# Hybrid encoder layer on one core: probability transposes issued in pairs of groups, gate transposes at the end of an iteration and in another PSUM bank pool

## The chip, the cores and the metric

One Trainium2 chip, one of its cores. The time is device microseconds for one execution of the whole kernel: one layer over 4096 tokens of width 1024. The engines are PE (TensorE, matmuls), DVE (VectorE), ACT (ScalarE), POOL (GpSimd) and SP (SyncE, which here only issues transfers). Each takes its own instructions in the order in which the built program lists them.

## The reference, cut to what matters

```python
h = rms(x) * norm_gain * (1 + scale) + shift          # scale, shift, gate = Linear(SiLU(c))
q, k, v, g_attn, u, v_gm, g_gm = split(h @ w_in)      # 8 query heads, 2 key/value heads of 64
s = rms(q) @ rms(k).T / 8 - slope * dist              # band of +-128 tokens, blocks of 128 queries
A = softmax([s, sink])[..., :-1] @ v * silu(g_attn)
M = u * (w_s @ rms(v_gm) + b_s) * silu(g_gm)          # chunks of 128 tokens
x = x + gate * (concat[A, M] @ w_out)
```

Float32 operands are split into a high and a low part (`h` and `l` in names), so that each product is three matmuls: high by high, low by high, high by low.

## The kernel before, in words

The work is done in three phases. Phase 1 makes query, key, value and attention gate of each of 32 blocks of 128 tokens and does the attention; it writes the attention half of the transposed, gated result to HBM. Phase 2 does the gMLP half, phase 3 the output product. The change touches phase 1 only.

Phase 1 is a loop, `run_iter(i)`, whose steady iterations are alike. The main work of iteration i is the projection of block i on PE: 24 matmuls of 256 columns for key and value (`pk`), 24 of 512 columns for the query (`pq`) and 24 of 512 for the gate (`pg`). Between them, `sides1(i)` inserts the attention of block a = i - 3 and preparations of other blocks. Each inserted step has a position, a fraction of the main work by the table `TUNE`; steps are sorted by position and issued when the main work has come that far.

The steps that matter here, for block a:

- `qk`, eight heads: two matmuls of 384 columns into a score tile `s` of the PSUM pool "s" (two banks); a DVE instruction at L551 adds the mask and takes the minimum (`mx`); ACT takes the exponential (L555). After the fourth and the eighth head `softmax` makes the denominators of those four on DVE (`es`, `den`, and the reciprocal at L568), and POOL scales the four probability tiles `pr` by them (L571).
- `pt_`, six groups, one for each key/value head j and key block q: four transposes on PE of four scaled probability tiles into one tile `pT` of the PSUM pool "t" (two banks), then ACT copies it to `ph` (L580) and DVE makes the rest `pl` (L581), which frees the bank.
- `pv_`, six groups: two matmuls of 512 columns that add probabilities times values into `po` of the pool "o".
- `tr_g`: four transposes of the gate tile `gf` into `gT`, before the change in a bank of the pool "s"; `finish1` multiplies the result `y` by it (L604), which frees that bank, and sends `y` to HBM from SP.
- `tr_q`, `tr_k` for block i - 1: four transposes of the query (`pqT`, pool "s") and one of the key (`pkT`, pool "t").
- `bg_bias2`, in 24 iterations: SP loads 256 KB of weights (`bgw`, L620) and DVE adds it, scaled, to a bias that phase 2 needs (L625 the first three times, L627 after that). It belongs to no block.

A scheduler then orders each engine's instructions by priority, which follows the order of issue in the code, and by its own estimate of when the inputs of each are there. So a step that moves on one engine can change the order on others. From iteration 29 on the PE's instructions are kept in the order of the code.

Of the kernel before, what the change touches and what calls it, by code (L numbers as in the profile page):

```python
# [8 lines left out]
F32 = mybir.dt.float32  # L9
# [7 lines left out]
P = 128  # L17
# [18 lines left out]
TUNE = dict(pin0=4, pin1=4, pinx=1, pinb=1, sqb=2, gfb=3, pk=3, pq=0, pg=0, bg0=4, vm=[[], ["v0", "v1", "g0", "g1",  # L36
            "v2"], ["v3", "g2", "g3"]], wg0=1.05, wgd=0.18, vn=0, vx=0.2, wv0=0.145, wvd=0.15,
            silu=0.45, ksplit=2, sb=["q1", "g0", "g1", "q0", "q2", "g2"], ch0=28, load=0.02, split=0.0,
            stats=0.525, bg=0.1, qk0=0.08, qkd=0.035, pt0=0.485, ptd=0.0715, pvlag=0.31, trg=0.5,
            fin=0.99, trk=0.93, trq=0.9, order="kqg", unch=0, hp2=30, hpx=0, qeng="V")  # L40


def body(tc, x, xT, c, cT, w_adaT, b_adaT, w_gate, b_gate, ngT, w_in, q_gain, k_gain, sink, wsT, bsT, w_out, out):
    nc = tc.nc
    V, A, G, T = nc.vector, nc.scalar, nc.gpsimd, nc.tensor
# [17 lines left out]
    def tr(ps, src):  # L63
        pe(T.transpose(ps, src, ident))  # L64
# [37 lines left out]
    def load_xT(pool, b, bufs=2, tail=False):  # L102
# [5 lines left out]
    ps_mm, ps_s, ps_t, ps_o = (  # L108
        ctx.enter_context(tc.tile_pool(name=f"ps_{t}", bufs=2, space=PSUM)) for t in ("mm", "s", "t", "o")
    )  # L110
# [165 lines left out]
    with tc.tile_pool(name="start", bufs=1) as st:  # L276
# [107 lines left out]
        for k in range(KC):  # L384
# [4 lines left out]
            t = base.tile([P, DA], F32, tag="qf", name=f"tg{k}", bufs=2)  # L389
# [131 lines left out]
    def slots(b):  # L521
        by = {(b + r) % 3: b + r for r in (-1, 0, 1) if 0 <= b + r < NB}
        s = sorted(by)
        assert s[-1] - s[0] + 1 == len(s)
        return by, s[0], s[-1] + 1
# [47 lines left out]
    def pt_(b, j, a):  # L573
        d = blk[b]
        pt = ps_t.tile([P, QPK, P], F32, tag="t", name=f"pT{b}_{j}_{a}")
        for i in range(QPK):
            tr(pt[:, i], d["pr", j][i][:, a])
        ph = base.tile([P, QPK, P], F32R, tag="ph", name=f"ph{b}_{j}_{a}", bufs=4)
        pl = base.tile([P, QPK, P], F32R, tag="pl", name=f"pl{b}_{j}_{a}", bufs=4)
        A.copy(ph, pt)  # L580
        V.tensor_tensor(pl, pt, ph.bitcast(F32), ALU.subtract)  # L581
        d["p", j, a] = ph, pl
# [19 lines left out]
    def finish1(b):  # L602
        d = blk[b]
        V.tensor_tensor(d["y"], d["y"], d["pg"], ALU.mult)  # L604
        (nc.scalar if b == NB - 1 else nc.sync).dma_start(yT[b][0], d["y"])

    def tr_g(b):
        d = blk[b]
        pt = ps_s.tile([P, 4, P], F32, tag="s", name=f"gT{b}")
        for i in range(4):  # L610
            tr(pt[:, i], d["gf"][:, i * P : (i + 1) * P])
        d["pg"] = pt
# [22 lines left out]
    def sides1(i):  # L635
        s = []

        def add(pos, f):
            s.append((pos, len(s), f))
# [12 lines left out]
        a = i - LAG  # L652
        if 0 <= a < NB:
            for b in range(NB):
                if i == max(b + LAG - 1, NS):
                    add(TUNE["silu"] if b > 1 else 0.0, lambda b=b: silu1([b]))
            _, s0, s1 = slots(a)
            for h in range(NH):
                add(TUNE["qk0"] + TUNE["qkd"] * h, lambda h=h: qk(a, h))
            seq = [(j, q) for j in range(NKV) for q in range(s0, s1)]  # L660
            for n, (j, q) in enumerate(seq):
                add(TUNE["pt0"] + TUNE["ptd"] * n, lambda j=j, q=q: pt_(a, j, q))
                add(TUNE["pt0"] + TUNE["ptd"] * n + TUNE["pvlag"], lambda j=j, q=q: pv_(a, j, q))
            add(TUNE["trg"], lambda: tr_g(a))
            add(max(TUNE["fin"], TUNE["pt0"] + TUNE["ptd"] * 5 + TUNE["pvlag"] + 0.001), lambda: finish1(a))
# [532 lines left out]
```

## Time and profile before

| | us |
|---|---|
| median of 3 runs | 1734.18 (1733.92 to 1738.13) |
| the profiled execution | 1734.84 |
| its span, first to last instruction | 1733.1 |
| phase 1, steady iterations (block 4 on) | from 113.0 on, 23.6 each |
| first matmul of phase 2's products inside the loop's tail | 783.7 |

Mean granted TensorE clock 0.990. Times in the rows below count from the start of the span. A row of the timeline is one instruction, or several equal ones in a row; matmul ends are modelled, so neighbouring matmuls overlap, and the pace of PE is read from start to start. The iteration shown below is that of block 23, from 562.19 to 585.82, with the attention of block 20.

### The profile page before, as it was taken

Reading aid. Unit: us, or ns where it says so; the run is one execution under the profiler, and the core shown is the slowest. Engines: PE = TensorE matmul, PEld = TensorE weight load, DVE = VectorE, ACT = ScalarE, POOL = GpSimd, SP = SyncE. Lnnn points to the kernel's source line nnn. Section 1 sums busy time; section 2 is a strip of 40 time slices with the busy share of each in tenths; the row PEclk is TensorE's granted clock in tenths of the full one; section 3 lists DMA queues with packets and bytes.
Section 4 is the critical chain, followed back from the end, with each engine's and each line's share of the span. In section 5 each row is a group of like instructions: output and inputs, shape, how many; then the busy total and the mean of one; then the engine's idle time right before and its main releaser. Section 6 shows DMA issues by size and latency. Waiting matters only on the chain.

```text
span 1733.1 us, 23001 instructions
## 1 busy us (share of the span) xinstructions
PE 1659.0 (96%) x8216; PEld 1370.8 (79%) x8216; DVE 1069.3 (62%) x2277; ACT 739.2 (43%) x1613; POOL 690.9 (40%) x612
## 2 busy tenths in 40 slices
PE   6789999999999999998989999998999989999999
PEld 4578888888888888876778888887888867888887
DVE  7987877787877787769773333355333456444443
ACT  3476666666666666656421212211122233222221
POOL 5653343443343443346422222222222337545552
PEclk9899999999999999999999999999999999999999
DMA  7522212222212222113250101136111146555442
GB/s 259 192 85 74 73 45 67 74 74 74 73 43 69 73 74 92 37 55 100 74 192 25 61 25 61 49 127 225 37 49 61 61 177 200 163 164 184 146 148 83
DMA packets 67762, 170.92 MB, mean 99 GB/s; under 512 B 8256, under 2 KB 8256, under 8 KB 67648
## 3 DMA queue, kind: packets, MB, share of 16 engines
q1 hardware_dynamic: 62896, 160.81, 27.9%
q10 hardware_dynamic: 4752, 8.65, 1.3%
q8 instruction: 64, 1.05, 0.3%
q14 instruction: 50, 0.41, 0.1%
HBM read 128.54 MB, written 40.89 MB: 98 GB/s over the span
## 4 chain that ended last, share of the span: by engine, by line
PE 78%; DVE 10%; ACT 2%; DMA 1%; issue 1%; POOL 1%; SPq 0%; POOLq 0%; DVEq 0%; ACTq 0%
PE pg L61 17%; PE pv L61 9%; PE pu L61 9%; PE pq L61 9%; PE oY L967 7%; PE oX L967 5%; PE oZ L967 5%; PE pT L64 5%; PE s L61 5%; PE po L61 3%; DVE y L600 2%; DVE pr L551 1%; PE sv L61 1%; PE pk L61 1%; DVE gf L495 1%
## 5 line engine op out<-in xcount | busy, mean ns | idle before, releaser
L97 POOL TENSOR_TENSOR xl<-xraw,xh 128x1024 fp32r<-128x1024 f32 x58 | 150.6, 2596 | 377.4 <-ACT xh L96 377.4
L571 POOL TENSOR_SCALAR pr<-pr,den 128x384 f32<-128x384 f32 (+1 forms) x256 | 146.4, 590 | 160.9 <-DVE vs L445 105.3
L555 ACT ACTIVATE pr<-pr,mx 128x384 f32<-128x384 f32 (+1 forms) x256 | 153.8, 601 | 59.0 <-DVE mx L551 58.3
L580 ACT CAST ph<-pT 128x512 fp32r<-128x512 f32 x188 | 109.7, 584 | 117.2 <-PE po L61 43.0
L551 DVE CUSTOM_DVE_ANT_0 pr<-s,negd,nsink 128x384 f32<-128x384 f32 (+1 forms) x256 | 152.5, 607 | 11.5 <-PE s L61 6.0
L61 PE MATMUL pu<-w2u,xh 128*128 128x512 f32 x480 | 148.8, 391 | 0.0
L61 PE MATMUL s<-kT,qT 128*128 128x384 f32 (+1 forms) x512 | 135.7, 346 | 12.8 <-DVE mx L551 11.7
L581 DVE TENSOR_TENSOR pl<-pT,ph 128x512 fp32r<-128x512 f32 x188 | 126.0, 685 | 15.6 <-ACT ph L580 15.6
L83 POOL TENSOR_TENSOR ssv<-ssv,mhalf 128x8 f32<-128x8 f32 x32 | 53.6, 1675 | 177.4 <-DVE ssv L82 177.2
L64 PE MATMUL pT<-ident,pr 128*128 128x128 f32 x752 | 115.9, 274 | 4.8 <-DVE pl L581 3.1
L64 PEld LDWEIGHTS pT<-ident,pr 128*128 128x128 f32 x752 | 93.3, 140 | 34.3 <-POOL pr L571 6.6
L61 PEld LDWEIGHTS s<-kT,qT 128*128 128x128 f32 x512 | 86.3, 188 | 33.4 <-DVE mx L551 20.6
L96 ACT CAST xh<-xraw 128x1024 fp32r<-128x1024 f32 x61 | 64.1, 1051 | 99.1 <-PE pu L61 97.0
L61 PEld LDWEIGHTS pu<-w2u,xh 128*128 128x128 f32 x480 | 91.0, 190 | 19.0
L61 PE MATMUL pg<-wgh,xl 128*128 128x512 f32 x232 | 98.4, 424 | 0.0
L61 PE MATMUL pg<-wgh,xh 128*128 128x512 f32 x232 | 98.2, 423 | 0.0
L61 PE MATMUL pu<-w2u,xl 128*128 128x512 f32 x240 | 94.3, 393 | 1.2 <-DVE xl L97 1.2
L61 PE MATMUL pq<-w1h,xh 128*128 128x512 f32 x232 | 94.1, 406 | 0.0
L61 PE MATMUL pq<-w1l,xh 128*128 128x512 f32 x232 | 93.8, 404 | 0.0
L61 PE MATMUL pq<-w1h,xl 128*128 128x512 f32 x232 | 91.9, 396 | 0.0
L61 PE MATMUL pg<-wgl,xh 128*128 128x512 f32 x232 | 91.5, 395 | 0.0
L61 PE MATMUL pv<-w2vh,xh 128*128 128x512 f32 x224 | 90.7, 405 | 0.0
(338 smaller groups left out, 4427.7 us busy)
## 6 DMA issues: line engine op xcount, KB each, us to landing
xraw<-xT SPq DMA_DIRECT2D x61, 512.0 KB, 4.0
xtok<-x SPq DMA_DIRECT2D x32, 512.0 KB, 5.0
yr<-yT SPq DMA_DIRECT2D x64, 256.0 KB, 4.1
xt<-x SPq DMA_DIRECT2D x32, 512.0 KB, 3.8
out<-xt SPq DMA_DIRECT2D x64, 256.0 KB, 3.5
wada<-w_adaT SPq DMA_DIRECT2D x16, 512.0 KB, 5.6
yT<-ybuf ACTq DMA_DIRECT2D x32, 256.0 KB, 2.2
yT<-y SPq DMA_DIRECT2D x31, 256.0 KB, 5.2
```

Source lines behind the costliest of these rows:

```text
L61: pe(T.matmul(ps, lhsT, rhs, start=start, stop=stop))
L64: pe(T.transpose(ps, src, ident))
L83: G.tensor_tensor(dst, dst, mhalf[:, :width], ALU.pow)
L96: A.copy(xh, xr)
L97: ins = eng.tensor_tensor(xl, xr, xh.bitcast(F32), ALU.subtract)
L551: V.tensor_tensor_reduce(flat(t[:, s0:s1]), flat(pss[:, s0:s1]), flat(negd[:, b % 3, s0:s1]), -(2.0 ** -(h + 1)), nsink[:, h : h + 1], ALU ...
L555: A.activation(t, t, AF.Exp, bias=m[:, i : i + 1], scale=-1.0, accum_out=d["den", j][:, i : i + 1])
L571: G.tensor_scalar(t, t, den[:, i : i + 1], 1.0, ALU.mult, ALU.mult)
L580: A.copy(ph, pt)
L581: V.tensor_tensor(pl, pt, ph.bitcast(F32), ALU.subtract)
L600: V.tensor_tensor(d["y"][e * HD : (e + 1) * HD, 2 * j : 2 * j + 2], po[:HD, e::2], lo[:, e::2], ALU.add)
L967: pe(T.matmul(ps, l[:, k], r[k], start=i < 3 and k == 0 and j == 0, stop=k == KC // 2 - 1 and j == 2, skip_group_check=i >= 3))
```

## The change

In the table, `trg` goes from 0.5 to 0.9 (gate transposes) and `trk` from 0.93 to 0.9 (key transpose). The positions of the six groups `pt_` are rounded so that groups 0 and 1, 2 and 3, 4 and 5 share one, half a step of 0.0715 behind that of the first. `pv_` keeps its positions. The tile of the gate's transposes comes from the pool "t" instead of "s".

```diff
-            stats=0.525, bg=0.1, qk0=0.08, qkd=0.035, pt0=0.485, ptd=0.0715, pvlag=0.31, trg=0.5,
-            fin=0.99, trk=0.93, trq=0.9, order="kqg", unch=0, hp2=30, hpx=0, qeng="V")
+            stats=0.525, bg=0.1, qk0=0.08, qkd=0.035, pt0=0.485, ptd=0.0715, pvlag=0.31, trg=0.9,
+            fin=0.99, trk=0.9, trq=0.9, order="kqg", unch=0, hp2=30, hpx=0, qeng="V")
...
     def tr_g(b):
         d = blk[b]
-        pt = ps_s.tile([P, 4, P], F32, tag="s", name=f"gT{b}")
+        pt = ps_t.tile([P, 4, P], F32, tag="t", name=f"gT{b}")
...
-                add(TUNE["pt0"] + TUNE["ptd"] * n, lambda j=j, q=q: pt_(a, j, q))
+                add(TUNE["pt0"] + TUNE["ptd"] * (n // 2 * 2 + 0.5), lambda j=j, q=q: pt_(a, j, q))
```

The number of instructions is the same on every engine; their order is not. DVE in the iteration of block 23, around the last two score tiles of block 20 (`s20_6`, `s20_7`), before; `den20_0` are the denominators of its first four heads:

```order
L568 RECIPROCAL den20_0_6506<-den20_0_6506 128x4
L445 SCALAR_TENSOR_TENSOR vs23_6562<-kvf23_6559,vs23_6562 128x2x64
L551 ISA pr20_6_6588,mx20_1_6567<-s20_6_6585,negd_196,nsink_199 128x384
L551 ISA mx20_1_6567 128x1
L551 ISA pr20_7_6596,mx20_1_6567<-s20_7_6593,negd_196,nsink_199 128x384
L551 ISA mx20_1_6567 128x1
L627 SCALAR_TENSOR_TENSOR bias2_141<-bgw19_6799,shift_136,bias2_141 128x512
L565 TENSOR_TENSOR es20_1_6599<-sinkb_200,mx20_1_6567 128x4
```

The same place now:

```order
L551 ISA pr20_6_6588,mx20_1_6567<-s20_6_6585,negd_196,nsink_199 128x384
L551 ISA mx20_1_6567 128x1
L567 TENSOR_TENSOR den20_0_6506<-den20_0_6506,es20_0_6547 128x4
L627 SCALAR_TENSOR_TENSOR bias2_141<-bgw19_6799,shift_136,bias2_141 128x512
L568 RECIPROCAL den20_0_6506<-den20_0_6506 128x4
L551 ISA pr20_7_6596,mx20_1_6567<-s20_7_6593,negd_196,nsink_199 128x384
L551 ISA mx20_1_6567 128x1
L82 TENSOR_SCALAR rstd_134<-rstd_134 128x1
L565 TENSOR_TENSOR es20_1_6599<-sinkb_200,mx20_1_6567 128x4
```

The bias instruction L627, which reads the loaded tile `bgw`, stood behind the eighth head's L551 and now stands ahead of it and of the reciprocal for the first four heads.

PE at the first probability transposes of the same iteration, before; `pT20_0_0` is the group of key/value head 0 and the first key block:

```order
L61 MATMUL pq23_6485<-w1h5_170,xl23_6204 128x512
L64 MATMUL pT20_0_0_6621<-ident_131,pr20_0_6510 128x128
L64 MATMUL pT20_0_0_6621<-ident_131,pr20_1_6523 128x128
L64 MATMUL pT20_0_0_6621<-ident_131,pr20_2_6533 128x128
L64 MATMUL pT20_0_0_6621<-ident_131,pr20_3_6544 128x128
L64 MATMUL gT20_6630<-ident_131,gf20_5901 128x128 x4
L61 MATMUL pq23_6485<-w1h6_172,xh23_6203 128x512
```

Now:

```order
L61 MATMUL pq23_6485<-w1h6_172,xh23_6203 128x512
L61 MATMUL pq23_6485<-w1l6_173,xh23_6203 128x512
L64 MATMUL pT20_0_0_6623<-ident_131,pr20_0_6510 128x128
L64 MATMUL pT20_0_0_6623<-ident_131,pr20_1_6523 128x128
L64 MATMUL pT20_0_0_6623<-ident_131,pr20_2_6533 128x128
L64 MATMUL pT20_0_0_6623<-ident_131,pr20_3_6544 128x128
L64 MATMUL pT20_0_1_6632<-ident_131,pr20_0_6510 128x128
L64 MATMUL pT20_0_1_6632<-ident_131,pr20_1_6523 128x128
L64 MATMUL pT20_0_1_6632<-ident_131,pr20_2_6533 128x128
L64 MATMUL pT20_0_1_6632<-ident_131,pr20_3_6544 128x128
```

The first group stands two `pq` matmuls later, the second group directly behind it, and the gate's transposes have left this place.

PE at the query's and key's transposes, before:

```order
L61 MATMUL pg23_6486<-wgl5_187,xh23_6203 128x512
L61 MATMUL pg23_6486<-wgh5_186,xl23_6204 128x512
L64 MATMUL pqT22_6723<-ident_131,qf22_6369 128x128 x4
L61 MATMUL pg23_6486<-wgh6_188,xh23_6203 128x512
L61 MATMUL pg23_6486<-wgl6_189,xh23_6203 128x512
L64 MATMUL pkT22_6734<-ident_131,kvf22_6275 128x128
L61 MATMUL pg23_6486<-wgh6_188,xl23_6204 128x512
```

Now:

```order
L61 MATMUL pg23_6486<-wgl5_187,xh23_6203 128x512
L61 MATMUL pg23_6486<-wgh5_186,xl23_6204 128x512
L64 MATMUL gT20_6717<-ident_131,gf20_5901 128x128 x4
L64 MATMUL pqT22_6731<-ident_131,qf22_6364 128x128 x3
L64 MATMUL pkT22_6722<-ident_131,kvf22_6275 128x128
L64 MATMUL pqT22_6731<-ident_131,qf22_6364 128x128
L61 MATMUL pg23_6486<-wgh6_188,xh23_6203 128x512
```

The gate's transposes now stand ahead of the query's, with the key's between them, behind the fifth and sixth probability groups, whose banks they take.

## Rows read from the trace of the kernel before

**Rows 1.** The page's head: span; busy time, share of the span and instructions by engine.

```profile
span 1733.1 us, 23001 instructions
...
PE 1659.0 (96%) x8216; PEld 1370.8 (79%) x8216; DVE 1069.3 (62%) x2277; ACT 739.2 (43%) x1613; POOL 690.9 (40%) x612
```

**Rows 2.** Waits of PE, whole span: for whom, us in total, times, longest.

```profile
PE s L61 <- DVE mx L551: 11.7, 31, 2.7
...
PE pT L64 <- POOL pr L571: 1.2, 5, 0.4
```

**Rows 3.** Windows view, block 23's iteration: length; busy us of PE, PEld, DVE, ACT, POOL; PEclk.

```profile
562.19:585.82 23.63, 23.43 (x135) 20.19 (x134) 18.84 (x51) 15.68 (x40) 9.46 (x11) 1.00 0.20 67
```

**Rows 4.** Timeline of PE, same iteration: start, duration, engine, line, instruction [idle before, releaser].

```profile
562.19 0.28 PE L61 MATMUL pk<-w1h,xh 128*128 128x256 f32 x1
...
565.07 0.62 PE L61 MATMUL s<-kT,qT 128*128 128x384 f32 x2 [0.20 <-DVE mx L551]
...
572.46 0.60 PE L64 MATMUL pT<-ident,pr 128*128 128x128 f32 x4
572.89 0.60 PE L64 MATMUL gT<-ident,gf 128*128 128x128 f32 x4
573.25 0.48 PE L61 MATMUL pq<-w1h,xh 128*128 128x512 f32 x1
573.57 0.40 PE L61 MATMUL pq<-w1l,xh 128*128 128x512 f32 x1
...
583.26 0.39 PE L61 MATMUL po<-ph,vs 128*128 128x512 f32 x1
...
585.82 0.28 PE L61 MATMUL pk<-w1h,xh 128*128 128x256 f32 x1
```

**Rows 5.** Timeline of DVE, same iteration.

```profile
570.79 0.62 DVE L551 CUSTOM_DVE_ANT_0 pr<-s,negd,nsink 128x384 f32<-128x384 f32 x1 [0.19 <-PE s L61]
...
572.18 0.75 DVE L627 SCALAR_TENSOR_TENSOR bias<-bgw,shift,bias 128x512 f32<-128x512 f32 x1 [0.77 <-DMA bgw<-w_in]
572.85 0.16 DVE L565 TENSOR_TENSOR es<-sinkb,mx 128x4 f32<-128x4 f32 x1
...
574.22 0.18 DVE L568 RECIPROCAL den<-den 128x4 f32<-128x4 f32 x1
...
575.37 0.75 DVE L457 SCALAR_TENSOR_TENSOR qf<-pq,rstd,bias 128x512 f32<-128x512 f32 x1
...
581.63 1.28 DVE L581 TENSOR_TENSOR pl<-pT,ph 128x512 fp32r<-128x512 f32 x2
```

**Rows 6.** Timeline of POOL, same iteration: the scaling of four tiles, twice.

```profile
569.92 2.28 POOL L571 TENSOR_SCALAR pr<-pr,den 128x384 f32<-128x384 f32 x4 [4.57 <-DVE vs L445]
...
574.57 2.27 POOL L571 TENSOR_SCALAR pr<-pr,den 128x384 f32<-128x384 f32 x4 [0.87 <-DVE den L568]
```

**Rows 7.** Timeline of SP, same iteration: issue of the transfer.

```profile
566.71 0.42 SPq L620 DMA_DIRECT2D bgw<-w_in  x1
```

**Rows 8.** Waits of DVE for that transfer, whole span.

```profile
DVE bias L627 <- DMA bgw<-w_in: 15.7, 21, 1.9
...
DVE bias L625 <- DMA bgw<-w_in: 2.4, 3, 1.0
```

**Rows 9.** The page's groups: the two reads that free a transpose's bank, count, busy, mean ns.

```profile
L580 ACT CAST ph<-pT 128x512 fp32r<-128x512 f32 x188 | 109.7, 584 | 117.2 <-PE po L61 43.0
...
L581 DVE TENSOR_TENSOR pl<-pT,ph 128x512 fp32r<-128x512 f32 x188 | 126.0, 685 | 15.6 <-ACT ph L580 15.6
```

**Rows 10.** Windows view, four neighbouring stretches in phase 3, columns as in rows 3.

```profile
1424.90:1428.30 3.40, 1.31 (x6) 1.08 (x7) 2.96 (x3) 0.81 (x2) 3.32 (x4) 1.00 1.03 411
1428.30:1431.70 3.40, 3.40 (x10) 2.63 (x9) 3.13 (x3) 2.13 (x5) 3.40 (x3) 0.50 0.19 74
1431.70:1435.10 3.40, 1.77 (x8) 1.07 (x7) 2.61 (x3) 2.10 (x5) 3.40 (x3) 1.00 0.00 0
1435.10:1438.50 3.40, 2.69 (x11) 1.88 (x11) 3.13 (x4) 1.40 (x3) 1.59 (x2) 1.00 0.27 67
```

## The prediction

> **What bounds the kernel now.** I read the page's head first: PE is busy for 1659.0 of 1733.1 us [rows 1]. The next view is the windows view of one steady iteration of phase 1: 23.43 of 23.63 us are PE's at full clock [rows 3]. So an iteration lasts as long as PE's own instructions, and the change, which leaves their number alone, can only take away waits of PE or add some. The list of waits says how much there is to take: in the whole span PE waits 11.7 us, in 31 pieces, for the score tiles' reads on DVE, and 1.2 us for scaled probabilities [rows 2]. The timeline of PE shows the piece that each iteration has: at 565.07 the second score tile waits because the gate's transposes hold one of the two banks of "s" and the first score tile the other [rows 4]. Read from start to start it is 0.35 us, more than the 0.20 of the row, since the end of a matmul is modelled.
>
> The other view that decides is DVE's timeline. At 572.18 the bias instruction L627 has waited 0.77 us for its transfer [rows 5]. That costs nothing now, since everything urgent stands ahead of it. The wait is there in nearly every iteration with such a transfer: 21 and 3 times, 0.75 us on the mean for the 21 [rows 8].
>
> **The change part by part.** Times below are counted from the start of the iteration, 562.19.
>
> *Pairing by itself* costs and saves PE nothing. Four transposes take 572.89 - 572.46 = 0.43 us, 0.11 each. Eight in a row with the first matmul behind them last from 572.46 to 573.57, 1.11, of which 0.23 are that matmul's: again 0.11 each [rows 4]. A 512-column matmul takes 0.233 (583.26 to 585.82, eleven of them) [rows 4].
>
> *The gate's tile leaving "s"* removes the 0.35 us wait of the second score tile, if DVE reads the tiles in time. 25 times 0.35 are 9 us, the most that this part can gain.
>
> *The bias instruction moved ahead of the reciprocal* is the large term. It still needs its transfer. SP issues that at 566.71 [rows 7], behind three others, and DVE starts on it at 572.18, 9.99 into the iteration. Neither SP's nor POOL's order changes in the steady iterations, and what holds the issue is a split on POOL at the iteration's start, so I take the start of L627 at 9.85; up to 0.3 earlier or 0.1 later is possible. Queued behind it on DVE are now the reciprocal for four heads, the eighth score tile, and so the denominators of the other four. From its start the next DVE instruction follows after 572.85 - 572.18 = 0.67 [rows 5], POOL starts 0.35 behind the reciprocal's start (574.22 [rows 5] to 574.57 [rows 6]), and scales four tiles in 2.28 [rows 6]. PE waits for these tiles one by one; its fourth transpose can start, with 0.05 for the hand-over, at 9.85 + 0.67 + 0.35 + 2.28 + 0.05 = 13.20. Before, the fourth started at 572.46 + 0.33 - 562.19 = 10.60 [rows 4], just behind tiles that POOL had ready at 572.20 (569.92 + 2.28, [rows 6]). Two more `pq` matmuls now stand ahead of it, 0.47, work that is only moved: 11.07 is the fair place. PE loses 13.20 - 11.07 = 2.13 us. This figure holds whatever becomes of the score tiles' waits before it, gain or loss, because the transfer sets the 13.20.
>
> *The gate's transposes behind the fifth group* need a bank of "t", hence the fifth group's read `pl` on DVE. Two paths lead from the fourth transpose at 13.20 to that place. PE: 21 transposes of 0.109 and 26 matmuls of 0.233, 8.34, so 21.54. DVE: transpose done at 13.47 (four take 0.60 with the last end, [rows 4]), first cast 0.58 and two reads of 0.69 each [rows 9], hand-overs included, then the query's evacuation at about 15.35. It now stands behind both reads of the pair and not behind one. From there to the end of the fifth group's read the chain (square, sum, power on POOL, scaling) took from 575.37 to 581.63 + 0.68 = 582.31, 6.94 [rows 5], so the bank is free at 22.29. PE waits 0.75. Bounds: 0.35 if the evacuation comes as early as PE's `pq` ends (14.97), 1.0 if ACT's casts slip by one.
>
> The rest of the iteration is unchanged work, so each iteration grows by 2.13 + 0.75 = 2.9 us, from 23.6 to 26.5. PE cannot make it up, having no slack [rows 3]; DVE and ACT have some.
>
> *Count.* There are 24 iterations with a transfer, 21 and 3 [rows 8]. In the first the order puts the bias instruction behind the first reciprocal, so that only the second four heads are late: about 1.4 us. 23 x 2.9 + 1.4 = 68. The three iterations after them have only the bank wait, some 0.7 each: 2. Phases 2 and 3 keep their order but for a few rows where phase 2 begins; I take 0 there, within 3 us either way. Together 70 us: 1734.84 of the profiled execution (span 1733.1 and 1.7 around it) becomes 1805; the median of the runs shown, 1734.18, lies 0.7 under the profiled one, so 1804 to 1805.
>
> *The clock.* PE now stands still for about 1.9 us within 2.6 us, in four pieces with single transposes between. In phase 3 the clock fell to half (0.50, which is 1.2 GHz) at 1428.3, after 3.40 us of which PE worked 1.31, and the next 3.40 us held ten matmuls; at 1435.1, after pauses that left PE 1.77 of 3.40, it stayed at 1.00 [rows 10]. No row has pauses like the new ones, in short pieces, so I allow for a fall now and then. One fall costs half of 3.40, 1.7 us. I add 2 us for one iteration in twenty and keep up to six falls, 10 us, for the range. Prediction: 1807.
>
> The Trainium skill (TensorE: Matmul & The Clock Gate, the section on a second failure mode, depth-cycling of PSUM queues) tells of a kernel in which short idle times between groups of matmuls, coming back in every round, made the clock swing between its two levels. By that rule each of the 23 iterations would lose another 1.7 us, and the kernel would come out at 1844; the rows of phase 3 show one case on either side, so it stands among the rivals.
>
> **The rivals.**
>
> *A. The clock falls in every iteration with a late transfer.* For it: the clock fell in phase 3 after a pause [rows 10]. Against: here the pause is broken by transposes, and the same rows have pauses after which the clock stayed. 1805 + 23 x 1.7 = 1844. Chance 0.06.
>
> *B. The transfer arrives in time and only the bank wait of the gate's transposes is left.* L627 would have to start by 13.20 - 11.07 = 2.13 earlier than 9.85. Then 27 x 0.75 less 25 x 0.35 give +11, and with the score tiles still waiting +20: 1746 to 1755. Against it: the transfer is the last of four issued together, and its wait hardly varies, 15.7 us in 21 pieces [rows 8]. Chance 0.04.
>
> *C. Faster: the "s" pool has two free banks and nothing else is late.* The mechanism is the 0.35 us of each iteration [rows 2, 4], 9 us in all, 1726. It decides if the transfer is there by 7.7 into the iteration and `pl` of the fifth group by 21.5 less what the pair comes earlier. DVE is busy for 18.84 of 23.63 us [rows 3], but the gate's SiLU and the final product now also stand ahead of the first score tile's read, so that even this wait may stay. Chance 0.02.
>
> That the change does nothing is excluded by the order of the instructions; a balance of gains and losses within 0.3% I give 0.01, that being about what a measurement here can tell from no change.
>
> **How the numbers follow.** The forecast, slower by 2.9 us in each of 23 iterations, has a chance of 0.87. Its low end: transfer 0.3 earlier and bank wait 0.35, 2.2 x 23 + 1 = 52, so 1786. Its high end: transfer 0.1 later, bank wait 1.0 and six clock falls, 3.25 x 23 + 6 + 10 = 91, so 1826. These bounds are the range, a little widened below for a part of B: 1780 to 1826. A lies above it, B and C below. Slower by over 0.3%: 0.87 + 0.06 + 0.04 = 0.97; same 0.01; faster 0.02.
>
> **What would show it.** Steady iterations of 26.5 us; DVE's wait for `bgw` twice as long in total as now, 30 us or more; in PE's waits a new leading line, transposes `pT` for POOL's `pr`, of some 35 us in 80 or more pieces (the modelled ends hide part of each); a line `gT` for DVE's `pl` of some 10 to 17 us; the fourth transpose of a pair at 13.2 into the iteration. If steady iterations last under 25 us, the transfer came early, or the eighth tile's place did not matter; if over 27.5, the clock or a wait I did not see has been added. The score tiles' wait may be gone or grow: it doesn't touch the sum in iterations with a transfer.

## The result, and the profile after

The changed kernel takes 1815.89 us (median of 4 runs, 1814.83 to 1816.86) against 1734.16 us of the kernel before (4 runs): 1.0459 times as long, 95% interval 1.0443 to 1.0475. 1807 was predicted.

The head of the page after, with the granted clock in 40 slices under it [rows 1]:

```profile
span 1813.0 us, 22978 instructions
...
PE 1680.5 (93%) x8216; PEld 1372.6 (76%) x8216; DVE 1090.3 (60%) x2277; ACT 731.8 (40%) x1613; POOL 690.2 (38%) x612
...
PEclk9899999999999999999999999999999999999999
```

The span grew by 79.9 us with the same number of matmuls, and the row of the granted clock is the kernel before's digit for digit: the time is waits of PE. In the list of PE's waits (for whom, us in total, times, longest) the first line has grown from 11.7 us, the second is new, and the third has grown from 1.2 [rows 2]:

```profile
PE s L61 <- DVE mx L551: 34.4, 30, 2.7
PE gT L64 <- DVE pl L581: 21.5, 28, 5.0
PE pT L64 <- POOL pr L571: 16.0, 67, 0.6
```

and DVE's waits for the bias step's transfer have hardly changed [rows 8]:

```profile
DVE bias L627 <- DMA bgw<-w_in: 15.2, 21, 1.6
DVE bias L625 <- DMA bgw<-w_in: 2.8, 3, 1.2
```

The loss lies in phase 1. Counted from the first `pk` matmul of each iteration, block 6 begins 6.1 us later than before. The next 22 iterations last 26.71 us on the mean instead of 23.64, 67.5 us together. Blocks 28 to 30, which run no bias step, add 6.2. The first matmul of phase 2's values then comes 79.6 us later, and the first of phase 3 still 79: the later phases are as they were. The windows view of a steady iteration, that of block 22 (that of block 23 in [rows 3] is its like), columns length, then busy us of PE, PEld, DVE, ACT and POOL, then the granted clock (the last two are DMA):

```profile
594.11:620.65 26.54, 24.23 (x134) 20.19 (x133) 19.71 (x51) 15.41 (x40) 9.42 (x11) 1.00 0.18 60
```

PE now idles 2.3 of 26.5 us at full clock, and DVE is busy 0.87 us longer with the same 51 instructions. PE's timeline shows where the idle time lies (start, duration, instruction; in brackets the idle time before it and what ended it) [rows 4]:

```profile
597.43 0.28 PE L61 MATMUL pk<-w1h,xl 128*128 128x256 f32 x1
598.92 0.62 PE L61 MATMUL s<-kT,qT 128*128 128x384 f32 x2 [1.21 <-DVE mx L551]
...
606.64 0.33 PE L64 MATMUL pT<-ident,pr 128*128 128x128 f32 x1 [0.23 <-POOL pr L571]
607.20 0.77 PE L64 MATMUL pT<-ident,pr 128*128 128x128 f32 x5 [0.23 <-POOL pr L571]
...
615.36 0.39 PE L61 MATMUL pg<-wgh,xl 128*128 128x512 f32 x1
616.38 0.66 PE L64 MATMUL gT<-ident,gf 128*128 128x128 f32 x4 [0.63 <-DVE pl L581]
```

There are three places: the third score tile (598.92), the first four transposes (the fourth starts at 607.20, 13.09 into this iteration) and the gate's transposes (616.38). DVE's timeline of the same iteration gives the reason for each [rows 5]:

```profile
596.43 1.30 DVE L536 SCALAR_TENSOR_TENSOR gf<-th,gf 128x512 f32<-128x512 f32 x1
597.65 0.68 DVE L604 TENSOR_TENSOR y<-y,gT 128x512 f32<-128x512 f32 x1
598.25 0.60 DVE L551 CUSTOM_DVE_ANT_0 pr<-s,negd,nsink 128x384 f32<-128x384 f32 x1
...
603.86 0.75 DVE L627 SCALAR_TENSOR_TENSOR bias<-bgw,shift,bias 128x512 f32<-128x512 f32 x1 [0.54 <-DMA bgw<-w_in]
604.53 0.17 DVE L568 RECIPROCAL den<-den 128x4 f32<-128x4 f32 x1
...
614.42 0.17 DVE L470 TENSOR_TENSOR ss<-ss,pow 128x10 f32<-128x10 f32 x1 [1.50 <-POOL ss L83]
...
614.83 0.68 DVE L491 TENSOR_TENSOR qf<-qf,ss 128x512 f32<-128x512 f32 x1
...
615.64 1.28 DVE L581 TENSOR_TENSOR pl<-pT,ph 128x512 fp32r<-128x512 f32 x2
```

The SiLU product L536 and the final product L604 stand ahead of the first score read L551, so the third score tile finds both banks of "s" taken. L627 waits for its transfer, but only 0.54 us, because DVE comes late itself; the first reciprocal stands behind it. The two reads `pl` that the gate's transposes wait for stand behind the query's and key's scaling.

Last, POOL's scaling and SP's issue [rows 6, 7]; POOL's first line of the iteration is a split (L97) that comes up again below:

```profile
594.77 2.41 POOL L97 TENSOR_TENSOR xl<-xraw,xh 128x1024 fp32r<-128x1024 f32 x1 [6.93 <-ACT xh L96]
604.88 2.27 POOL L571 TENSOR_SCALAR pr<-pr,den 128x384 f32<-128x384 f32 x4 [7.70 <-DVE den L568]
```

```profile
598.35 0.33 SPq L605 DMA_DIRECT2D yT<-y  x1
598.73 0.42 SPq L620 DMA_DIRECT2D bgw<-w_in  x1
```

The transfer is issued 4.62 us into the iteration (4.52 before). What it stands behind has changed: SP sends `y` first, and `y` is ready only when L604 ends, at 598.33. In the kernel before, L604 had ended 0.67 us before SP came to `y`:

```profile
564.92 0.68 DVE L604 TENSOR_TENSOR y<-y,gT 128x512 f32<-128x512 f32 x1
...
566.27 0.38 SPq L605 DMA_DIRECT2D yT<-y  x1
```

So DVE's late product now also holds the transfer that L627 waits for.

### The profile page after: what moved, and what is told of

The parts are those of the page before. It is cut to its first block, busy times and chain, and to the rows that moved or that the text cites. A ratio compares the mean times of both kernels' runs of the same rounds, so it can differ in the third digit from the quotient of the medians.

```text
span 1813.0 us, 22978 instructions
## 1 busy us (share of the span) xinstructions
PE 1680.5 (93%) x8216; PEld 1372.6 (76%) x8216; DVE 1090.3 (60%) x2277; ACT 731.8 (40%) x1613; POOL 690.2 (38%) x612
## 4 chain that ended last, share of the span: by engine, by line
PE 46%; DVE 3%; POOL 2%; DMA 2%; ACT 1%; issue 1%; SPq 0%; POOLq 0%; DVEq 0%; ACTq 0%
PE pv L61 9%; PE pg L61 9%; PE pu L61 9%; PE oY L967 7%; PE oX L967 5%; PE oZ L967 5%; PE sv L61 1%; PE yT L64 1%; DMA stT<-wB_T 1%; POOL pr L571 0%; DMA wg<-w_gate 0%; DVE pr L551 0%; PE po L61 0%; PE pT L64 0%; DVE vl L819 0%
## 5 line engine op out<-in xcount | busy, mean ns | idle before, releaser
L97 POOL TENSOR_TENSOR xl<-xraw,xh 128x1024 fp32r<-128x1024 f32 x58 | 151.2, 2607 | 396.4 <-ACT xh L96 396.4
L580 ACT CAST ph<-pT 128x512 fp32r<-128x512 f32 x188 | 103.5, 585 | 129.7 <-PE pT L64 109.6
L551 DVE CUSTOM_DVE_ANT_0 pr<-s,negd,nsink 128x384 f32<-128x384 f32 (+1 forms) x256 | 148.7, 602 | 9.2 <-PE s L61 6.8
L64 PEld LDWEIGHTS pT<-ident,pr 128*128 128x128 f32 x752 | 87.7, 140 | 51.9 <-POOL pr L571 39.2
L61 PEld LDWEIGHTS pu<-w2u,xh 128*128 128x128 f32 x480 | 90.7, 189 | 21.5 <-issue 2.8
L61 PE MATMUL pg<-wgl,xh 128*128 128x512 f32 x232 | 95.9, 414 | 0.0
L61 PE MATMUL pg<-wgh,xh 128*128 128x512 f32 x232 | 93.8, 404 | 0.0
L83 POOL TENSOR_TENSOR ss<-ss,mhalf 128x10 f32<-128x10 f32 (+2 forms) x34 | 63.9, 1879 | 76.5 <-DVE ss L82 76.3
L61 PE MATMUL pg<-wgh,xl 128*128 128x512 f32 x232 | 91.2, 393 | 0.0
```

Source lines behind the costliest of these rows:

```text
L61: pe(T.matmul(ps, lhsT, rhs, start=start, stop=stop))
L83: G.tensor_tensor(dst, dst, mhalf[:, :width], ALU.pow)
L97: ins = eng.tensor_tensor(xl, xr, xh.bitcast(F32), ALU.subtract)
L551: V.tensor_tensor_reduce(flat(t[:, s0:s1]), flat(pss[:, s0:s1]), flat(negd[:, b % 3, s0:s1]), -(2.0 ** -(h + 1)), nsink[:, h : h + 1], ALU ...
```

## The experiments

All times in this table but the last column are means over 18 steady iterations (blocks 9 to 26), read from each run's trace, in us from the iteration's first `pk` matmul. "Place" is the start of the fourth transpose of the probabilities. Beside the experiments the kernel before took 1735.9 to 1736.4 us; each ratio below is against those runs.

| kernel | period | L627 starts | first reciprocal | place | time, us |
|---|---|---|---|---|---|
| before | 23.64 | 9.98 | 7.38 | 10.59 | 1734.2 |
| changed | 26.72 | 9.93 | 10.60 | 13.26 | 1815.9 |
| pairs only | 23.69 | 9.92 | 7.38 | 11.48 | 1736.4 |
| gate only | 26.71 | 9.89 | 10.55 | 13.23 | 1808.6 |
| changed, gate in its old bank | 25.93 | 9.55 | 10.22 | 12.89 | 1788.2 |
| changed, bias step later | 25.99 | 12.06 | 9.85 | 12.53 | 1802.2 |
| changed, SiLU later | 25.28 | 9.99 | 7.30 | 11.10 | 1783.6 |
| SiLU later, bias step first, data there | 25.29 | 8.14 | 8.80 | 11.47 | 1783.1 |
| SiLU later, bias step first, it waits | 27.16 | 10.01 | 10.68 | 13.35 | 1825.8 |
| changed, weights asked for earlier | 26.56 | 9.77 | 10.44 | 13.10 | 1812.0 |
| changed, SiLU and square later | 25.15 | 19.47 | 7.30 | 11.10 | 1778.1 |
| rebuilt | 23.95 | 9.67 | 6.94 | 10.05 | 1745.7 |
| rebuilt, square later | 23.13 | 19.33 | 6.94 | 10.05 | 1724.8 |
| the same in pairs | 23.70 | 18.90 | 6.94 | 10.53 | 1738.3 |

### Pairs alone

```diff
-                add(TUNE["pt0"] + TUNE["ptd"] * n, lambda j=j, q=q: pt_(a, j, q))
+                add(TUNE["pt0"] + TUNE["ptd"] * (n // 2 * 2 + 0.5), lambda j=j, q=q: pt_(a, j, q))
```

> The kernel before with the pairing alone: the gate's transposes stay where they were and in their old bank. Theory (the loss comes from where the bias step and the score reads stand on VectorE, which only the gate's move changed): VectorE's order is that of the kernel before but for one pair of pl subtractions, so the fourth transpose of the first pair starts some 10.6 us into a steady iteration as before and the period stays near 23.6 us: 1734 to 1745 us. Rival (groups of eight transposes in a row cost TensorE, by their own turnover of the two t tiles): most of the 82 us shows here, 1790 us or more.

Measured: 1736.41 us, ratio 1.0001 (0.9986 to 1.0015). A steady iteration by the windows view, columns as above:

```profile
563.20:586.80 23.60, 23.42 (x135) 20.25 (x134) 18.67 (x51) 15.44 (x40) 9.48 (x11) 1.00 0.20 68
```

PE is as full as before [rows 3]. The place is 11.48 and not 10.6, because two `pq` matmuls, 0.47 us, and the gate's four transposes, 0.45 us, here stand ahead of it. The theory holds: pairing alone costs nothing.

### The gate alone

```diff
-            stats=0.525, ..., trg=0.5, fin=0.99, trk=0.93, trq=0.9,
+            stats=0.525, ..., trg=0.9, fin=0.99, trk=0.9, trq=0.9,
...
-        pt = ps_s.tile([P, 4, P], F32, tag="s", name=f"gT{b}")
+        pt = ps_t.tile([P, 4, P], F32, tag="t", name=f"gT{b}")
```

> The gate's move and its new bank alone, groups of four transposes spread as before. Theory: VectorE's order is that of the changed kernel (bias step ahead of the first reciprocal, silu and finish ahead of the first score read), so the fourth transpose of the iteration's first group still starts near 13.2 us and the gate's transposes still wait for a pl: 1800 to 1816 us. Rival (the pairs are needed for the loss, since a lone group of four can be slipped in later): 1735 to 1765 us.

Measured: 1808.58 us, ratio 1.0418 (1.0402 to 1.0433). The steady period is that of the changed kernel, 26.71 us. What the pairs add to it, 7 us, does not lie in the steady iterations. So the move of the gate, with the key's new position, carries the loss.

### The gate in its old bank, at its new place

```diff
-        pt = ps_t.tile([P, 4, P], F32, tag="t", name=f"gT{b}")
+        pt = ps_s.tile([P, 4, P], F32, tag="s", name=f"gT{b}")
```

> The changed kernel with the gate's transposes back in the score tiles' bank, at their new place at the end of the iteration. Theory (two separate prices, 2.1 to 2.6 us in the first pair and 0.8 us at the gate's transposes): the first stays, fourth transpose near 13.2 us; of the second the four transposes (0.45 us) now run while the subtraction is waited for, and the key's transpose behind them waits for what is left, 0.3 us: 28 x 0.45 = 12 us less than the changed kernel, 1800 to 1806 us. Rival 1 (the bank is the main price): 1750 us or less. Rival 2 (the gate's wait only moves to the next transposes in that bank): 1816 us.

Measured: 1788.24 us, ratio 1.0306 (1.0291 to 1.0321); 28 us less than the changed kernel where 12 were expected. The waits of PE:

```profile
PE s L61 <- DVE y L604: 26.5, 27, 2.5
PE pT L64 <- POOL pr L571: 14.8, 62, 0.7
...
PE pkT L64 <- DVE pl L581: 4.8, 26, 0.2
```

The gate's wait is gone, as the theory had it, and the key's transpose waits 0.2 us. But the place came 0.37 us earlier too, where the theory had it stay. DVE's first stretch begins earlier, counted from the first `pk` matmul (SiLU at 1.99 instead of 2.32), L604 ends at 3.88 instead of 4.21, and the transfer behind it is issued at 4.29 instead of 4.63 and lands 0.4 us earlier. The two prices are not separate: the gate's wait comes back in the next iteration. The wait for a score tile only changed its releaser; now the gate's tile holds the bank until L604.

### The bias step behind the second reciprocal

```diff
-            stats=0.525, bg=0.1, ...
+            stats=0.525, bg=0.33, ...
...
-            V.scalar_tensor_tensor(acc, w, shift[:, k : k + 1], acc, ALU.mult, ALU.add)
+            tc.keep_in_program_order(V.scalar_tensor_tensor(acc, w, shift[:, k : k + 1], acc, ALU.mult, ALU.add))
```

> The changed kernel with only the bias step moved, behind the second reciprocal on VectorE, by when its data have landed. Theory (the bias step's wait and its 0.76 us stand ahead of the reciprocal that the first pair waits for): VectorE reached that step 0.5 us before the data landed, so the reciprocal comes 0.5 + 0.76 us earlier, less up to 0.6 us for the last score read that now stands ahead of it: the fourth transpose near 12 to 12.6 us, 0.7 to 1.3 us less in 25 iterations, 1784 to 1798 us; the rest of the loss is the wait for a score tile and the gate's. Rival 1 (the transfer is the whole 2.1 us, as the prediction priced it): 1766 us or less. Rival 2 (the wait for score tiles sets the pair, the transfer hides beside it): 1812 to 1816 us.

Measured: 1802.16 us, ratio 1.0384 (1.0368 to 1.0399), 14 us less than the changed kernel. DVE's timeline, last score read, first reciprocal and bias step, in the iteration that starts at 582.05:

```profile
591.36 0.62 DVE L551 CUSTOM_DVE_ANT_0 pr<-s,negd,nsink 128x384 f32<-128x384 f32 x1
591.90 0.17 DVE L568 RECIPROCAL den<-den 128x4 f32<-128x4 f32 x1
...
594.10 0.96 DVE L627 SCALAR_TENSOR_TENSOR bias<-bgw,shift,bias 128x512 f32<-128x512 f32 x1
```

The place moved by 0.73 us, from 13.26 to 12.53, the low end of the 0.7 to 1.3 us expected; the time is 4 us above its range, and 3 of these lie in two iterations without a bias step (blocks 29 and 30, 28.7 and 26.8 us long). The first reciprocal still comes at 9.85, because the score reads themselves are late. No transfer plays a part in that: each step here takes the data loaded an iteration earlier. So in the changed kernel the bias step is not alone in holding the pair. "The transfer is the whole 2.1 us" falls.

### SiLU behind the third score read

```diff
-                V.scalar_tensor_tensor(g, t, 1.0, g, ALU.add, ALU.mult)
+                tc.keep_in_program_order(V.scalar_tensor_tensor(g, t, 1.0, g, ALU.add, ALU.mult))
...
-                if i == max(b + LAG - 1, NS):
-                    add(TUNE["silu"] if b > 1 else 0.0, lambda b=b: silu1([b]))
+                if i == max(b + LAG - 2 + (b == NB - 1), NS):
+                    add(0.16 if b > 2 else 0.0, lambda b=b: silu1([b]))
```

> The changed kernel with one VectorE instruction moved: the next block's silu multiplication (L536) is held behind the third score read instead of standing ahead of the first. VectorE's order then falls back to that of the kernel before also for the finish (behind the first score read) and the bias step (behind the eighth); the pairs, the gate's place and its bank stay as changed. Theory (what costs the time is the order of VectorE's first stretch, in two places that the silu's place decides): the fourth transpose near 11 us, the gate's wait of 0.4 to 0.8 us in each of 28 iterations stays, the score tiles' 0.35 us goes: 1734 + 11 to 22 - 9, 1736 to 1748 us. Rival (the gate's new place and bank cost by themselves, whatever the order on VectorE): 1790 us or more.

Measured: 1783.56 us, ratio 1.0273 (1.0259 to 1.0288). Half right. The order fell back as intended, the place is 11.10, and the third score tile waits 0.24 us instead of 1.36. But the period is 25.28 us, 1.6 above that of pairs alone, and the time 36 us over the expected range. Two waits follow behind the pair: 0.70 us at the gate, as expected, and 0.65 us in the fourth group, which waits for POOL's second four tiles. The second reciprocal comes at 12.40 here and at 11.93 with pairs alone. ACT's timeline shows why (iteration from 570.5):

```profile
579.01 1.06 ACT L164 ACTIVATE xtok<-xtok 128x1024 f32<-128x1024 f32 x1 [1.52 <-DMA xtok<-x]
...
580.07 0.60 ACT L555 ACTIVATE pr<-pr,mx 128x384 f32<-128x384 f32 x1
...
581.87 0.60 ACT L555 ACTIVATE pr<-pr,mx 128x384 f32<-128x384 f32 x1
```

The square of the x rows waits for its own transfer with four exponentials queued behind it; in the kernel before there are three. The same kind of cost stands on a second engine.

### The bias step first, with its data there and without

Two kernels on top of the last one, both with the order of score reads, SiLU and final product of the kernel before, and the bias step ahead of the first reciprocal. The first:

```diff
-            stats=0.525, bg=0.1, ...
+            stats=0.525, bg=0.2905, ...
+            if 4 < i < 29:
+                add(0.291, lambda: blk[a]["rec"]())
...
-            V.scalar_tensor_tensor(acc, w, shift[:, k : k + 1], acc, ALU.mult, ALU.add)
+            tc.keep_in_program_order(V.scalar_tensor_tensor(acc, w, shift[:, k : k + 1], acc, ALU.mult, ALU.add))
```

where `rec` is the reciprocal and the scaling of heads 0 to 3, cut out of `softmax`, with the reciprocal kept in program order.

> As the run with the silu held back, but the bias step is put ahead of the first reciprocal again, behind the seventh score read, where the changed kernel has it; score reads, silu and finish stay in the order of the kernel before. So the bias step's transfer is the only thing that can hold the first pair. Theory (the transfer alone is enough, as the prediction had it; the late score reads lie beside it): the bias step starts near 9.9 us, the fourth transpose at 13.1 to 13.3 us, 1795 to 1814 us. Rival (the late score reads are the cause, the transfer costs only what it adds behind them, 0.7 us): 1750 to 1770 us.

Measured: 1783.12 us, ratio 1.0271 (1.0252 to 1.0290). It did not test what it was built for: the pinned step takes the data that were loaded an iteration earlier and never waits:

```profile
578.48 0.75 DVE L638 SCALAR_TENSOR_TENSOR bias<-bgw,shift,bias 128x512 f32<-128x512 f32 x1
579.14 0.17 DVE L577 RECIPROCAL den<-den 128x4 f32<-128x4 f32 x1
```

What it does show is the price of the instruction without its wait: the place moves by 0.37 us, to 11.47, and the period not at all. The second kernel brings the wait back, by issuing the transfer only when a small memset behind the third score read has run:

```diff
+        tc.keep_in_program_order(V.memset(w[:, 0:1], 0.0))
         ins = nc.sync.dma_start(w, w_in[k * P : (k + 1) * P, C1 + c0 : C1 + c0 + 512])
...
-                add(TUNE["bg"] + 0.3 * (n - n0), lambda n=n: bg_bias2(n))
+                add(0.151, lambda n=n: bg_bias2(n))
+                add(TUNE["bg"], lambda n=n: bg_use(n))
```

> The run with the bias step ahead of the first reciprocal once more. There the pin had put the step on data loaded an iteration earlier, so it never waited (it started at 8.1 us). Now its transfer is issued in the same iteration, behind a one-column memset on VectorE that stands behind the third score read (some 4.5 us in), so that it lands 9.6 to 10 us into the iteration, as in the changed kernel; score reads, silu and finish keep the order of the kernel before. Theory (the transfer alone is enough for what the prediction priced): the bias step starts at 9.6 to 10 us, the fourth transpose at 13.0 to 13.4 us against 11.5 in that run, 1.5 to 1.9 us in 24 iterations on top of its 1783 us: 1819 to 1829 us, or less where the later waits (0.65 us for scaled probabilities, 0.7 us at the gate) hide in it: 1803 at the least. Rival (the transfer's wait costs nothing of its own): 1780 to 1788 us.

Measured: 1825.80 us, ratio 1.0516 (1.0498 to 1.0534), inside the theory's range. DVE, and PE's transposes, in the iteration from 598.5:

```profile
608.41 0.75 DVE L649 SCALAR_TENSOR_TENSOR bias<-bgw,shift,bias 128x512 f32<-128x512 f32 x1 [1.65 <-DMA bgw<-w_in]
609.08 0.17 DVE L577 RECIPROCAL den<-den 128x4 f32<-128x4 f32 x1
```

```profile
610.07 0.33 PE L64 MATMUL pT<-ident,pr 128*128 128x128 f32 x1 [0.59 <-POOL pr L582]
...
611.75 0.90 PE L64 MATMUL pT<-ident,pr 128*128 128x128 f32 x5 [0.23 <-POOL pr L582]
```

The place is at 13.35 with every score read early. The transfer alone is enough for the whole shift that the prediction gave it; between the two kernels it costs 13.35 - 11.47 = 1.88 us. And here, without the other wait beside it, the two signatures stand that the prediction named and the changed kernel does not have: L627's wait is 36.8 us in 21 pieces, the transposes' wait for POOL 34.0 us in 102.

The clock also answers here. The windows view of this run, two neighbouring iterations and a stretch of the second, behind the fourth transpose:

```profile
571.80:598.50 26.70, 24.67 (x134) 20.31 (x133) 18.80 (x52) 15.47 (x40) 9.43 (x11) 1.00 0.18 60
598.50:626.10 27.60, 26.21 (x134) 21.48 (x133) 19.14 (x52) 15.67 (x40) 9.43 (x11) 0.94 0.18 58
...
612.25:615.65 3.40, 3.40 (x11) 2.72 (x10) 2.04 (x3) 1.49 (x3) 2.22 (x4) 0.50 0.00 0
```

In 10 iterations of this kernel the period is over 27.4 us and not some 26.5. In eight of them the granted clock falls behind four waits at the first four transposes, which by starts are 0.75 and three times 0.45 us in the iteration shown: to 0.50, the 1.2 GHz level, in the stretch shown. In the other two (blocks 17 and 18) it stays at 1.00, and the transfer lands some 0.9 us later than usual. In most iterations, the one from 571.8 among them, four such waits leave the clock at 1.00. Rival A of the prediction is real in this kernel, with some 1.1 us a fall instead of 1.7, and in 8 of 24 iterations. What decides between them, these rows do not tell.

### The weights asked for an iteration earlier

The transfer's issue is cut out of `bg_bias2` and put into the iteration before:

```diff
+            n0, n1 = (3 * KC * max(n - TUNE["bg0"], 0) // (29 - TUNE["bg0"]) for n in (i + 1, i + 2))
+            for n in range(n0, n1):
+                add(TUNE["bg"] + 0.001, lambda n=n: bg_load(n))
```

> The changed kernel, all orders kept, with the bias step's weights loaded one iteration ahead, so that the step never waits for them. Theory (two waits beside each other, the score reads' and the transfer's): VectorE reaches the step 0.5 us before it started in the changed kernel, the fourth transpose near 12.7 us, 24 x 0.5 = 12 us less, 1798 to 1806 us. Rival 1 (the transfer is the whole 2.1 us): 1766 us or less. Rival 2 (it costs nothing, the score reads set all): 1814 to 1818 us.

Measured: 1812.02 us, ratio 1.0440 (1.0422 to 1.0458). Inconclusive, and this is the line that says so:

```profile
598.77 0.75 DVE L636 SCALAR_TENSOR_TENSOR bias<-bgw,shift,bias 128x512 f32<-128x512 f32 x1 [0.56 <-DMA bgw<-w_in]
```

The step still waits. The scheduler moved it forward together with its transfer: from block 5 on, the steps stand one iteration earlier, each in the iteration of its own transfer, so nothing was taken away. That it came out near the expectation of rival 2 means nothing.

### A rebuilt kernel, and its square

The kernel before, without pairs, with three edits: the gate's tile in "t" at the end of the iteration (`trg=0.97`, behind the query's and key's), SiLU as above, and the final product carried over to the next iteration:

```diff
+        if late:
+            add(0.12, late.pop())
...
+            if a < 28:
+                late.append(lambda: finish1(a, True))
```

> Built from the readings: the kernel before without pairs, with the gate's transposes in the other bank but at the end of the iteration, behind the query's and key's, the silu held behind the third score read and the finish carried over to the next iteration behind the second score read. Theory: the 0.35 us at the second score tile goes in some 25 iterations, since no gate tile stands in its bank, the gate's transposes find a free tile, and the bias step stays behind the eighth score read: 1734 - 9 = 1725 us (1722 to 1729). Rival 1 (the score tiles then wait for VectorE as long as they did for the bank): 1732 to 1738 us. Rival 2 (the gate's transposes still wait for a subtraction): 1740 us or more.

Measured: 1745.71 us, ratio 1.0057 (1.0044 to 1.0069). Slower than before, against the theory; the time is in rival 2's range, but the wait is at another place. The score tiles wait no more, the place is at 10.05, and then PE runs into the next wait:

```profile
559.83 0.66 PE L64 MATMUL pT<-ident,pr 128*128 128x128 f32 x4 [0.46 <-DVE pl L581]
```

The third group needs the tile of the first. The copy of that tile on ACT stands behind the four exponentials that queue behind ACT's square, and its read on DVE behind the second reciprocal, which waits for the same exponentials (second reciprocal at 12.08). So the next kernel moves the square too:

```diff
-        A.activation(xt, xt, AF.Square, accum_out=rstd[:, b : b + 1])
+        tc.keep_in_program_order(A.activation(xt, xt, AF.Square, accum_out=rstd[:, b : b + 1]))
...
-            add(TUNE["stats"], lambda: stats1(i + 1))
+        for b in [4] * (i == NS) + [i + 2] * (i + 2 < NB):
+            add(0.56, lambda b=b: stats1(b))
```

> The run built from the readings, with one more step moved: ScalarE's square of the x rows (L164), which waits for their transfer until 8.5 us into an iteration with four exponentials queued behind it, now stands behind the second copy of the transposed probabilities. Theory: the exponentials of heads 4 to 7 start as soon as their scores are read, the second reciprocal comes some 1 us earlier (near 11 us against 12.1), the first pl subtraction with it, and the third group's 0.6 us wait goes: a period of 23.3 us, 1722 to 1730 us. Rival 1 (the square then delays the copies, and the groups behind wait instead): 1740 us or more. Rival 2 (no gain left beside the kernel before): 1732 to 1738 us.

Measured: 1724.80 us, ratio 0.9937 (0.9923 to 0.9951): inside the theory's range, and 0.6% below the kernel before, clear of the interval. The windows view of one iteration:

```profile
554.82:577.94 23.12, 23.12 (x135) 19.96 (x134) 18.68 (x51) 15.77 (x40) 9.48 (x11) 1.00 0.20 69
```

PE is busy for all of it, so a shorter iteration would need less work on PE. The bias step went with the square, from 9.67 to 19.33: SP issues its transfer behind that of the x rows, which now waits for the later square. That is not where the gain comes from: in the kernel without this edit, DVE stood idle for 1.48 us behind the bias step, waiting for the exponentials.

### The square moved in the changed kernel, and pairs in the fastest one

> The changed kernel with two steps moved: the silu behind the third score read, as in the run with that alone, and ScalarE's square of the x rows behind the second copy of transposed probabilities. Pairs, the gate's place and its bank are those of the changed kernel. Theory (all of the loss but the gate's own wait comes from the two orders): the 0.65 us wait of the fourth group for scaled probabilities goes, the gate's transposes still wait 0.7 us for a pl: a period near 24.2 to 24.6 us, 1752 to 1764 us. Rival 1 (the gate's wait goes as well, since the subtractions come earlier): 1728 to 1742 us. Rival 2 (the square does not matter here): 1780 us or more.

Measured: 1778.12 us, ratio 1.0241 (1.0226 to 1.0257), only 5 us less than with SiLU alone. The fourth group waits no more, as expected, yet the gate's wait has grown:

```profile
PE gT L64 <- DVE pl L581: 36.6, 29, 3.6
```

```profile
559.15 0.69 DVE L491 TENSOR_TENSOR qf<-qf,ss 128x512 f32<-128x512 f32 x1
...
559.96 0.75 DVE L627 SCALAR_TENSOR_TENSOR bias<-bgw,shift,bias 128x512 f32<-128x512 f32 x1
560.62 1.28 DVE L581 TENSOR_TENSOR pl<-pT,ph 128x512 fp32r<-128x512 f32 x2
```

The bias step, its transfer again issued late behind the x rows', now stands in the one gap that matters, ahead of the read that frees the gate's tile. By starts the wait grows from 0.70 to 1.43 us, about what the step holds DVE. The iteration of block 28, which has no bias step, lasts 24.49 us, as the theory had it for all. None of the three forecasts of the time held, but the run shows what the gate waits for: DVE's chain, not PE's.

> The fastest kernel so far (1725 us) with the pairs added. Theory (pairs cost TensorE nothing where the probabilities are there in time): the period stays near 23.1 to 23.2 us, 1723 to 1728 us. Rival (the pair behind the last score tiles asks for its probabilities and its free tile too early): 1732 us or more.

Measured: 1738.26 us, ratio 1.0007 (0.9998 to 1.0016): 13 us more than without pairs. The theory falls, and it is the rival's case, if at another place:

```profile
PE pkT L64 <- DVE pl L581: 9.0, 22, 1.1
```

The last pair is transposed together, its two reads run together behind the scaling and the bias step, and the key's transpose, which asks for one of the tiles, waits 0.53 us by starts in each iteration. In the iteration of block 28, which has no bias step, the period is 23.10 us, and without pairs 23.17: there the pairs cost nothing. Pairs are free only as long as the next user of "t" does not ask before the second read is done, and here it is the bias step ahead of the reads that makes it ask too early.

## Why the prediction came out as it did

**The pairs.** Right: nothing, by the run with pairs alone.

**The gate's tile leaving "s".** Its condition, that DVE reads the tiles in time, failed. The second score tile waits no more, but the third waits 1.36 us by starts, because SiLU and the final product now stand ahead of all score reads. The prediction saw both, took nothing for them and held that this "doesn't touch the sum in iterations with a transfer". There that came out: place and gate's wait together make 2.96 of the 3.07 us that such an iteration grew by.

**The bias step.** The number was right: L627 starts at 9.93 (predicted 9.85), the fourth transpose at 13.26 (13.20), and the kernel in which the transfer is the only late thing has it at 13.35. These two bear out the claim that the figure holds whatever becomes of the score tiles, as long as the transfer's issue stays where it is. That it stayed is in part luck. The prediction had the issue held by the split on POOL, which ends 0.1 us earlier than before (3.07); in the changed kernel SP waits for L604 instead (4.21), so the issue comes at 4.63, 4.58 before. Where L604 ended earlier, with the gate in its old bank, the place came down to 12.89. As a cause in the changed kernel the transfer is half of the truth. Two waits lie beside each other, and against the fair place of 11.07, the fourth transposes of four kernels are (upper row: SiLU later, and bias step later; lower row: SiLU later with the bias step first and waiting, and the changed kernel):

| | score reads early | score reads late |
|---|---|---|
| bias step does not hold the pair | 11.10 | 12.53 |
| it holds the pair and waits | 13.35 | 13.26 |

Either one costs 1.4 to 2.3 us alone, both together 2.2. That is why the signatures failed: DVE reaches L627 late, so its wait did not double (15.2 us, 30 or more expected), and PE, held up earlier at the third score tile, asks for its transposes later (16.0 us in 67 pieces, 35 in 80 or more expected). A reader who had gone by these signatures alone would have thrown out the right number.

**The gate's transposes.** Right: 0.77 us by starts, 0.75 predicted, at 22.27 in the iteration above, 22.29 predicted. The chain was the one on DVE, as the run with the bias step in it shows. The line `gT` has 21.5 us, above the 10 to 17 expected, because of one wait of 5.0 us at 916, behind the loop's steady part; the other 27 pieces are 16.5 us. The 15.35 for the query's evacuation is 15.43 by the durations that the prediction names; the trace has 15.28.

**The count.** 22 iterations at 3.07 us instead of 2.9 give 3.7 us more. The term that was mis-sized is the iterations without a bias step: 2.3, 2.1 and 1.7 us instead of 0.7 each, and 2.0 in that of block 3, for which nothing was counted. That is 6 us more, and with the 3.7 the 70 us of the sum become the 80 of the traces. In the three iterations without a bias step no transfer sets the place, and the score tiles' wait, which the sum left out, is paid besides the gate's: 1.2, 1.0 and 0.6 us in PE's rows. The run with the bias step later bears it out: with no transfer left to wait for, its steady iterations still last 25.99 us, 2.35 more than before.

**The clock.** The 2 us allowed were not used: 1.00 in steady iterations. The fall exists, but in a kernel with longer waits in one place. The Trainium skill (TensorE: Matmul & The Clock Gate, the section on a second failure mode, depth-cycling of PSUM queues) describes a clock that swings with such recurring gaps; here that is seen in 8 iterations of one kernel, and in none of the steady ones of the changed kernel.

**Phases 2 and 3.** Right, within 1 us.

What stays open: why the iteration of block 3 loses 2.0 us, and what the pairs' 7 us outside the steady iterations are. In block 3's iteration the first score tile waits 2.97 us for the copy of the transposed query (0.68 before, where a later one waits 1.47 for a score read), and the granted clock is 0.95 on the mean (1.00 before); with pairs alone it is 0.94 there, and nothing is lost, so the clock by itself does not explain it.

## What to carry to other kernels

Where an engine runs its queue in order, an instruction that waits for a transfer charges its wait to everything behind it, so read each queue for such instructions ahead of what the busiest engine needs; this kernel had one on DVE and one on ACT. When a wait looks like the cause, take it away and also leave it as the only one: of two waits beside each other, each looks small as long as the other stays. And a freed microsecond goes to the next engine's order, which a scheduler may choose anew, so look at the order after each edit; the gain here came only when the square, too, was out of the way.

## What was not expected of the hardware

L536 took 1.30 us in the changed kernel and not 0.69. The groups of DVE's lines from 160 to 700 us, first of the changed kernel, then of the kernel before (busy us, mean ns):

```profile
L536 DVE SCALAR_TENSOR_TENSOR gf<-th,gf 128x512 f32<-128x512 f32 x20 | 25.8, 1292 | 0.6
```

```profile
L536 DVE SCALAR_TENSOR_TENSOR gf<-th,gf 128x512 f32<-128x512 f32 x23 | 15.8, 689 | 0.0
```

In the iteration shown of the changed kernel it runs from 596.43 to 597.73, and POOL's split L97 until 597.18; all 26 that start beside the split take 1.28 to 1.30. In the kernel before, and in the run with SiLU behind the third score read, it starts after the split has ended, and takes 0.69. Both operands of L536 lie in SBUF. The final product L604, which reads PSUM, ran beside the split in the kernel before and took 0.68 as ever. The bias step, with its operands in SBUF, took 0.96 instead of 0.75 where it ran beside POOL's scaling. The time shows as a longer instruction, not as idle time, so no list of waits has it. It adds 0.6 us to the late score reads.

The Trainium skill (SBUF — State Buffer, the section SBUF: two separate sides) states that a DVE instruction with two inputs in SBUF and a GpSimd instruction that reads SBUF lock each other out, and that the loser blocks until the other has ended. The trace agrees in kind; L536 ended 0.55 us after the split, a little sooner than its own 0.69.
